# Two of a pair's four sums of weight blocks made by DMA

## The chip, the cores and the metric

The kernel runs on one core of a Trainium2 chip. The time is the device time of one execution in microseconds (us); the median of several executions is compared.

## The reference

The reference is a small decoder trunk for 512 positions of width 1024 in float32: a recurrent layer (Griffin RG-LRU) and a layer of stick-breaking attention, with a feed-forward block ahead of and behind each. The four feed-forward blocks are what the change is about. Each computes, for a hidden width of 2816,

```python
def swiglu(h, w13, w2):
    gate, up = jnp.split(h @ w13, 2, axis=-1)
    return (jax.nn.silu(gate) * up) @ w2
```

on an RMS-normed `h`, and half of the result is added to the residual stream.

## The kernel before, in words

Everything is kept transposed: 128 partitions of features by 512 positions. A product in float32 precision is made of three passes of TensorE: a weight tile is split into a high part (`hi`, rounded to the format that TensorE takes) and a low part (`lo`, the raw tile minus `hi`), the activations likewise, and `hi*hi`, `hi*lo` and `lo*hi` are added up in PSUM.

The hidden width of a feed-forward block is cut into 22 columns of 128, taken in three parts of 8, 8 and 6 (`THIRDS`). Some first columns of a block are computed plainly (`PLAIN`: 6, 4, 0 and 4 in the four blocks). All others are taken two at a time, as **pairs**: gate and up of two columns form one matrix, which is multiplied by Strassen's scheme in Winograd's form with seven products of half size instead of eight (`pair`, `FORMS`). There are 37 pairs. Behind each third stand the eight down products with `w2`.

A pair's seven weights are called forms and are used in the order a11, a12, s2, s3, s1, a22, s4. Four of them would be blocks of the weights (a11, a12, a22, and a21, which is only used in sums); the sums are s1 = a21 + a22, s2 = s1 + a11, s3 = a11 + a21 and s4 = s2 + a12 (`SUMS`). A block is a tile of 128x1024 float32, 512 KB. For each form the engines do this:

- SP's queue loads the block from HBM (L109), or VectorE adds two tiles (L114);
- ScalarE casts the tile to `hi` (L85), VectorE subtracts to get `lo` (L89);
- TensorE does 24 matmuls of 128x256 with them (L201).

The results of the forms are gathered in three PSUM banks, X, Y and Z. The forms a11, s2, s1 and s4 all add to bank X; between them ScalarE or VectorE takes out what has been added up so far (L389 to L399), then come Silu (L401, L402), the product of gate and up (L403, L404) and the split of the activations (L409, L410).

`Weights` deals out the tiles. Its plan lists all weights in the order of use. `get` returns the next one, and before that it emits loads, sums and splits of those ahead: in the feed-forward blocks up to four ahead. When a pair's first form is emitted, `block` issues all four loads of the pair at once and makes the sums when their form is asked for. Raw tiles come from two pools that have seven buffers together (three and four), `hi` and `lo` from pools of five; a load or a sum waits until a buffer of its pool is free. The order of instructions on each engine is laid down when the program is built, by a scheduler that goes by data dependences, free buffers and the order of emission; on the chip each engine works its list off in that order. GpSimd works at the start, in the recurrent layer, with k and q, and in attention; its casts of weights (L87) and subtraction (L89) belong to the start and to those layers.

Of the kernel before, what the change touches and what calls it, by code (L numbers as in the profile page):

```python
# [10 lines left out]
ALU = mybir.AluOpType  # L11
# [11 lines left out]
BLOCKS = ("a11", "a21", "a22", "a12")  # L23
SUMS = {"s3": ("a11", "a21"), "s1": ("a21", "a22"), "s2": ("s1", "a11"), "s4": ("s2", "a12"), **{b: None for b in BLOCKS}}
# [24 lines left out]
class Weights:  # L49
# [53 lines left out]
    def block(self, j, name, src):  # L103

        g = self.group
        if not g:
            for k, b in enumerate(BLOCKS):
                g[b] = self.tile(j, "w_raw", f"w_{b}_{j}")
                self.nc.sync.dma_start(g[b], src[k])  # L109
        if name not in g:  # L110
            p, q = SUMS[name]
            p, q = (self.block(j, t, src) for t in (p, q))
            g[name] = self.tile(j, "w_raw", f"w_{name}_{j}")
            self.nc.vector.tensor_tensor(out=g[name], in0=p, in1=q, op=ALU.add)  # L114
        return g[name]
# [960 lines left out]
```

## Time and profile before

| | |
|---|---|
| median of 3 runs | 1880.0 us (1879.47 to 1881.92) |
| the profiled execution, its own time | 1879.02 us |
| its span, first to last instruction | 1877.3 us |
| mean granted clock of TensorE | 0.994 of full speed |
| TensorE busy | 1839.0 us |
| VectorE busy | 1382.4 us |
| ScalarE busy | 921.7 us |
| GpSimd busy | 156.6 us |
| moved by DMA | 207.87 MB |

The profile is of one execution. In its rows PE is TensorE's matmuls, PEld its weight loads, DVE is VectorE, ACT ScalarE, POOL GpSimd, SP the engine whose queue issues the loads (SPq). A row of an instruction shows `out<-in` by the names of the tiles, shapes as partitions x elements, `xN` for N of them, and in brackets the idle time of the engine just before it with what ended it. `w_a` is a tile with a block, `w_s` one with a sum, `w_hi` and `w_lo` the split parts. Times in a row of the timeline count from the start of the span.

### The profile page before, as it was taken

Reading aid. Unit: us, or ns where it says so; the run is one execution under the profiler, and the core shown is the slowest. Engines: PE = TensorE matmul, PEld = TensorE weight load, DVE = VectorE, ACT = ScalarE, POOL = GpSimd, SP = SyncE. Lnnn points to the kernel's source line nnn. Section 1 sums busy time; section 2 is a strip of 40 time slices with the busy share of each in tenths; the row PEclk is TensorE's granted clock in tenths of the full one; section 3 lists DMA queues with packets and bytes.
Section 4 is the critical chain, followed back from the end, with each engine's and each line's share of the span. In section 5 each row is a group of like instructions: output and inputs, shape, how many; then the busy total and the mean of one; then the engine's idle time right before and its main releaser. Section 6 shows DMA issues by size and latency. Waiting matters only on the chain.

```text
span 1877.3 us, 27297 instructions
## 1 busy us (share of the span) xinstructions
PE 1839.0 (98%) x11040; PEld 1633.1 (87%) x11040; DVE 1382.4 (74%) x1709; ACT 921.7 (49%) x1282; POOL 156.6 (8%) x196
## 2 busy tenths in 40 slices
PE   9999999999999999999899999999898999999999
PEld 7889989778789899997689899898676789899897
DVE  8958657698788586576978667585799879667483
ACT  6525435368555254354545335254588745345251
POOL 1000000032000000000200000000365500000000
PEclk9999999999999999999999999999999999999999
DMA  6223423222415134232474324134365431425131
GB/s 225 91 79 98 139 71 98 79 79 82 154 46 179 46 101 124 90 93 76 135 213 126 111 79 146 56 111 148 117 188 154 147 92 46 146 79 157 57 109 61
DMA packets 73118, 207.87 MB, mean 111 GB/s; under 512 B 7584, under 2 KB 17056, under 8 KB 72480
## 3 DMA queue, kind: packets, MB, share of 16 engines
q1 hardware_dynamic: 72704, 205.81, 35.3%
q8 instruction: 86, 1.41, 0.3%
q10 hardware_dynamic: 288, 0.32, 0.1%
q14 instruction: 40, 0.33, 0.1%
HBM read 189.85 MB, written 16.25 MB: 110 GB/s over the span
## 4 chain that ended last, share of the span: by engine, by line
PE 44%; DVE 5%; issue 3%; POOL 2%; ACT 1%; SPq 0%; DMA 0%; POOLq 0%; DVEq 0%; ACTq 0%
PE pdffn L201 13%; PE pXffn L201 12%; PE pYffn L201 6%; PE pZffn L201 3%; PE v L201 2%; PE wo L201 2%; PE k L201 2%; PE puffn L201 1%; PE pgffn L201 1%; DVE spl L862 1%; PE z L201 1%; DVE t L862 1%; DVE sp L852 1%; POOL sph L859 0%; DVE w_lo L89 0%
## 5 line engine op out<-in xcount | busy, mean ns | idle before, releaser
L85 ACT CAST w_hi<-w_raw 128x1024 fp32r<-128x1024 f32 (+1 forms) x165 | 165.7, 1007 | 256.5 <-PE pdffn L201 82.5
L85 ACT CAST w_hi<-w_s 128x1024 fp32r<-128x1024 f32 x148 | 155.2, 1050 | 254.0 <-PE pdffn L201 105.4
L89 DVE TENSOR_TENSOR w_lo<-w_raw,w_hi 128x1024 fp32r<-128x1024 f32 (+3 forms) x191 | 219.9, 1154 | 76.8 <-ACT w_hi L85 68.2
L201 PE MATMUL pXffn<-hhffn,w_hi 128*128 128x256 f32 x832 | 235.5, 283 | 0.3 <-ACT effn L389 0.3
L201 PE MATMUL pXffn<-hlffn,w_hi 128*128 128x256 f32 x832 | 235.5, 283 | 0.0
L201 PE MATMUL pXffn<-hhffn,w_lo 128*128 128x256 f32 x832 | 235.5, 283 | 0.0
L201 PE MATMUL pdffn<-ahffn,w_hi 128*128 128x512 f32 x592 | 230.8, 390 | 0.3
L201 PE MATMUL pdffn<-alffn,w_hi 128*128 128x512 f32 x592 | 230.7, 390 | 0.0
L201 PE MATMUL pdffn<-ahffn,w_lo 128*128 128x512 f32 x592 | 230.4, 389 | 0.0
L89 DVE TENSOR_TENSOR w_lo<-w_s,w_hi 128x1024 fp32r<-128x1024 f32 x148 | 180.8, 1221 | 33.1 <-ACT w_hi L85 33.0
L85 ACT CAST w_hi<-w_a 128x1024 fp32r<-128x1024 f32 x111 | 116.5, 1050 | 171.4 <-PE pdffn L201 70.2
L89 DVE TENSOR_TENSOR w_lo<-w_a,w_hi 128x1024 fp32r<-128x1024 f32 x111 | 135.5, 1222 | 36.2 <-ACT w_hi L85 34.8
L201 PEld LDWEIGHTS pXffn<-hhffn,w_hi 128*128 128x128 f32 x832 | 159.7, 192 | 0.8 <-ACT effn L389 0.5
L201 PEld LDWEIGHTS pXffn<-hlffn,w_hi 128*128 128x128 f32 x832 | 159.7, 192 | 0.3
L201 PEld LDWEIGHTS pXffn<-hhffn,w_lo 128*128 128x128 f32 x832 | 159.7, 192 | 0.0
L453 DVE SCALAR_TENSOR_TENSOR x<-pdffn,x 128x512 f32<-128x512 f32 x72 | 49.8, 691 | 141.2 <-PE pdffn L201 141.2
L201 PEld LDWEIGHTS pdffn<-ahffn,w_hi 128*128 128x128 f32 x592 | 111.2, 188 | 24.6 <-ACT ahffn L409 1.8
L201 PEld LDWEIGHTS pdffn<-alffn,w_hi 128*128 128x128 f32 x592 | 111.2, 188 | 24.4 <-DVE alffn L410 1.1
L201 PEld LDWEIGHTS pdffn<-ahffn,w_lo 128*128 128x128 f32 x592 | 111.2, 188 | 22.7
L201 PE MATMUL pYffn<-hhffn,w_hi 128*128 128x256 f32 x416 | 117.7, 283 | 0.0
L201 PE MATMUL pYffn<-hlffn,w_hi 128*128 128x256 f32 x416 | 117.7, 283 | 0.0
L201 PE MATMUL pYffn<-hhffn,w_lo 128*128 128x256 f32 x416 | 117.7, 283 | 0.0
(1154 smaller groups left out, 4691.7 us busy)
## 6 DMA issues: line engine op xcount, KB each, us to landing
w_a<-in_ffn_s SPq DMA_DIRECT2D x148, 512.0 KB, 3.7
w_raw<-in_ffn_w SPq DMA_DIRECT2D x90, 512.0 KB, 4.5
w_raw<-in_ffn_w SPq DMA_DIRECT2D x32, 384.0 KB, 3.4
w_raw<-in_w_in SPq DMA_DIRECT2D x16, 512.0 KB, 3.6
qp<-qd SPq DMA_DIRECT2D x14, 512.0 KB, 5.5
w_raw<-in_w_out SPq DMA_DIRECT2D x8, 512.0 KB, 3.8
w_raw<-in_w_k SPq DMA_DIRECT2D x8, 512.0 KB, 3.6
w_raw<-in_w_v SPq DMA_DIRECT2D x8, 512.0 KB, 3.7
```

The costliest lines, as they stand in the source:

```text
L85: nc.scalar.copy(out=hi[:, cs], in_=raw[:, cs])
L89: eng.tensor_tensor(out=lo[:, cs], in0=raw[:, cs], in1=hi[:, cs].bitcast(F32), op=ALU.subtract)
L201: nc.tensor.matmul(o, l, r, start=start, stop=stop, skip_group_check=True)
L453: nc.vector.scalar_tensor_tensor(out=x[m], in0=pd, scalar=0.5, in1=x[m], op0=ALU.mult, op1=ALU.add)
L852: nc.vector.scalar_tensor_tensor(out=self.sp, in0=self.z, scalar=0.0, in1=ee, op0=ALU.max, op1=ALU.add)
L862: nc.vector.tensor_tensor(out=lo, in0=src, in1=hi.bitcast(F32), op=ALU.subtract)
```

## The change

When a pair's first form is emitted, five tiles are loaded in place of four, in the order a11, a12, s1, a22, s3. The tile of s1 is loaded with a21, and a DMA on GpSimd's queue then reads a22 from HBM and adds it to the tile; the tile of s3 is loaded with a11, and a second DMA adds a21. The sums s2 and s4 stay adds on VectorE. No tile holds a21 any more, so a pair has seven raw tiles instead of eight. From HBM a pair reads seven blocks instead of four.

```diff
@@ -104,12 +104,15 @@
         g = self.group
         if not g:
-            for k, b in enumerate(BLOCKS):
+            for b in ("a11", "a12", "s1", "a22", "s3"):
                 g[b] = self.tile(j, "w_raw", f"w_{b}_{j}")
-                self.nc.sync.dma_start(g[b], src[k])
+                p, q = SUMS[b] or (b, None)
+                self.nc.sync.dma_start(g[b], src[BLOCKS.index(p)])
+                if q:
+
+                    self.nc.gpsimd.dma_start(g[b], src[BLOCKS.index(q)], accum_op=ALU.add)
         if name not in g:
-            p, q = SUMS[name]
-            p, q = (self.block(j, t, src) for t in (p, q))
+            p, q = (g[t] for t in SUMS[name])
             g[name] = self.tile(j, "w_raw", f"w_{name}_{j}")
             self.nc.vector.tensor_tensor(out=g[name], in0=p, in1=q, op=ALU.add)
         return g[name]
```

## Rows read from the trace of the kernel before

**Rows 1.** The page: span; busy time, share of the span and instructions by engine.

```profile
span 1877.3 us, 27297 instructions
...
PE 1839.0 (98%) x11040; PEld 1633.1 (87%) x11040; DVE 1382.4 (74%) x1709; ACT 921.7 (49%) x1282; POOL 156.6 (8%) x196
```

**Rows 2.** By stretch: length; PE, PEld, DVE, ACT, POOL busy; clock, DMA share, GB/s.

```profile
520.00:835.00 315.00, 314.74 (x2098) 291.11 (x2097) 226.30 (x258) 141.40 (x178) 0.00 (x0) 1.00 0.31 96
835.00:971.00 136.00, 128.10 (x546) 103.17 (x545) 104.86 (x149) 66.85 (x99) 14.02 (x16) 0.97 0.43 136
...
1572.00:1840.00 268.00, 268.00 (x1893) 252.84 (x1892) 186.06 (x195) 115.02 (x143) 0.00 (x0) 1.00 0.34 107
...
1011.38:1031.54 20.16, 20.16 (x170) 20.16 (x170) 17.06 (x19) 10.86 (x15) 0.00 (x0) 1.00 0.35 106
```

**Rows 3.** Chain that ended last, in two stretches: start us, us, what.

```profile
1008.50 5.76 PE pXffn L201 x48
...
1017.14 2.88 PE pXffn L201 x24
...
1598.02 2.88 PE pXffn L201 x24
```

**Rows 4.** Timeline of ScalarE in an ordinary pair and in a pair behind plain columns.

```profile
1015.07 0.58 ACT L389 COPY effn<-pXffn 128x512 f32<-128x512 f32 x1
...
1028.62 1.05 ACT L85 CAST w_hi<-w_s 128x1024 fp32r<-128x1024 f32 x1 [1.83 <-PE pYffn L201]
...
1031.51 1.05 ACT L85 CAST w_hi<-w_s 128x1024 fp32r<-128x1024 f32 x1 [1.10 <-PE pXffn L201]
...
1590.11 1.05 ACT L85 CAST w_hi<-w_s 128x1024 fp32r<-128x1024 f32 x1 [4.34 <-DVE w_s L114]
...
1595.06 1.05 ACT L85 CAST w_hi<-w_a 128x1024 fp32r<-128x1024 f32 x1 [0.92 <-PE pXffn L201]
...
1597.05 0.57 ACT L389 COPY effn<-pXffn 128x512 f32<-128x512 f32 x1
```

**Rows 5.** Groups by line: sums of two blocks; busy us, mean ns, idle us before and its releasers.

```profile
L114 DVE TENSOR_TENSOR w_s<-w_a,w_a 128x1024 f32<-128x1024 f32 x74 | 90.0, 1221 | 13.4 <-DMA w_a<-in_ffn_s 11.3 <-issue 1.4
```

**Rows 6.** Waits of SP's queue: waiting line, what ended it, us, times, longest us.

```profile
SPq L109 <- DVE w_lo L89: 539.3, 98, 21.3
```

**Rows 7.** Timeline of SP's queue ahead of the pairs at 1031.54 and 1592.27.

```profile
1004.00 7.13 SPq L109 DMA_DIRECT2D w_a<-in_ffn_s  x4
...
1007.96 0.33 SPq L109 DMA_DIRECT2D w_a<-in_ffn_s  x1
...
1572.57 9.01 SPq L109 DMA_DIRECT2D w_a<-in_ffn_s  x4
...
1579.55 0.80 SPq L109 DMA_DIRECT2D w_a<-in_ffn_s  x2
1579.93 1.65 SPq L109 DMA_DIRECT2D w_a<-in_ffn_s  x2
```

**Rows 8.** Groups on GpSimd: busy us, mean ns, idle us before and its releasers.

```profile
L87 POOL TENSOR_SCALAR w_hi<-w_raw 128x1024 fp32r<-128x1024 f32 x17 | 20.0, 1176 | 706.4 <-PE pdffn L201 678.2 <-issue 11.5 <-PE q L201 9.3
...
L675 POOL TENSOR_SCALAR thk<-tk 128x512 fp32r<-128x512 f32 x8 | 7.5, 944 | 419.6 <-ACT tk L672 419.6
...
L89 POOL TENSOR_TENSOR w_lo<-w_raw,w_hi 128x1024 fp32r<-128x1024 f32 x1 | 2.7, 2677 | 0.1
...
L324 POOL TENSOR_SCALAR o0h<-o 128x512 fp32r<-128x512 f32 x1 | 0.6, 615 | 0.0
```

**Rows 9.** The tile `w_a`: time from issue to landing of its loads.

```profile
DMA to landing us min/median/max: 3.2/3.7/7.1
```

**Rows 10.** Timeline of VectorE in the pair from 1011.38.

```profile
1015.41 1.23 DVE L114 TENSOR_TENSOR w_s<-w_a,w_a 128x1024 f32<-128x1024 f32 x1 [1.42 <-issue]
...
1020.62 1.22 DVE L114 TENSOR_TENSOR w_s<-w_s,w_a 128x1024 f32<-128x1024 f32 x1
...
1028.70 0.69 DVE L399 TENSOR_TENSOR effn<-pYffn,effn 128x512 f32<-128x512 f32 x1 [0.58 <-PE pYffn L201]
```

## The prediction

> **What bounds the kernel now.** I read the page first: of a span of 1877.3 us TensorE is busy 1839.0, VectorE 1382.4, GpSimd 156.6 [rows 1]. A busy share is an average over unlike stages, so next I cut the span into stretches [rows 2]. Where the pairs run, TensorE is busy all the time: 314.74 of 315.00 us in one feed-forward block, 268.00 of 268.00 in the last, 20.16 of 20.16 in a single pair, at a granted clock of 1.00, the upper of its two levels (2.4 GHz). What it idles lies elsewhere, for instance in the k and v products (128.10 of 136.00), where the change edits nothing. The chain of waits shows why [rows 3]: in a pair one form of 24 matmuls follows the other at 2.88 us, and seven make 20.16 us. So in the 37 pairs TensorE is the bound, and VectorE, with 17.06 us of work in those 20.16 [rows 2], lies beside it.
>
> One order must still be seen, for ScalarE works in line. It casts the raw blocks and also copies the first form out of its PSUM bank (L389). TensorE's third form adds to that same bank, so the copy has to be done before it starts. In the pair that starts at 1011.38, halfway through the first row of [rows 3], the copy starts at 1015.07 and takes 0.58 us [rows 4]; the third form starts at 1017.14: 1.49 us to spare. A late cast ahead of a copy in ScalarE's line is thus the way from a late block to TensorE.
>
> **What is removed.** Two of four adds per pair, those of two blocks: 74 at 1.221 us, 90.0 us of VectorE [rows 5]. They lie where TensorE has no idle time to give back (0.26 us in the stretches read), so I take 0. Their tiles go or move too: 7 raw tiles per pair where there were 8, over the same 7 buffers. The last sum of a pair no longer waits for a buffer of its own pair, and SP's loads, which wait mostly for VectorE's splits to free one (539.3 us in 98 waits) [rows 6], should start no later than now.
>
> **What is added: one load.** Five loads of 512 KB per pair on SP's queue in place of four. An issue is 0.33 us [rows 7], five are 1.65 of 20.16; SP waits for buffers anyway. Four loads now keep the 16 DMA engines 0.35 busy over a pair [rows 2], 1.76 us of all engines per load; the fifth makes it 0.44.
>
> **What is added: two accumulating DMAs on GpSimd's queue.** GpSimd does nothing in the stretches with pairs [rows 2]; its next casts wait for the down products in any case (678.2 us) [rows 8]. Behind a waiting accumulation stands only the other one. It waits first for its load to land: 3.7 us from issue, median, 7.1 at most [rows 9]. Then GpSimd has to issue, which no row shows: from 0.33 us, SP's issue [rows 7], to 2.7, GpSimd's longest operation on a tile of 128x1024; I take 1.2, what its cast of such a tile takes [rows 8]. The transfer, which reads two operands and writes one, no row shows either: no less than a plain load, 3.7 us; at most two of the slowest loads end to end, 14.2. I take 2 x 3.7 = 7.4, two ordinary transfers, the nearest to the work. So issue and transfer are 8.6 us (bounds 4.0 and 16.9). On the engines an accumulation at one to two plain loads brings a pair's share from 0.44 to between 0.61 and 0.79: no queue fills up.
>
> **Is that hidden?** Take the pair that runs from 1031.54, 20.16 after the one above. Its four loads go out from 1004.00 on, the third at 1007.96 [rows 7]. Put in that place, s1 is summed at 1007.96 + 3.7 + 8.6 = 1020.3, just ahead of where s2's add stands, 1020.62 [rows 10]. The fifth load (for s3) can have its buffer by 1015.41, when the first sum takes one today [rows 10]: 1015.41 + 12.3 = 1027.7, and its cast is at 1028.62 [rows 4]. A later cast is absorbed too: before its next cast ScalarE idles 1.10 us [rows 4], and the copy has its 1.49 to spare, together 2.6. Issue and transfer may so take 1028.62 + 2.6 - 1015.41 - 3.7 = 12.1 us before TensorE waits. Cost in an ordinary pair: 0.
>
> Tightest is the second pair behind the plain columns, which two feed-forward blocks have in the same form; I read the later one. Its loads come at 1572.57 and then three from 1579.55 on, the second of these at 1579.93 [rows 7], and ScalarE already waits 4.34 us for a sum before 1590.11 [rows 4]. A third load at 1579.93 makes s1 at 1592.2 and s2 at 1593.5, its cast 3.4 us late. Behind it stand 0.92 us of idle time and the copy, which ends at 1597.62, 0.40 ahead of the third form [rows 3, 4]: TensorE would lose 3.4 - 0.92 - 0.40 = 2.1 us. Against that, its buffers come free earlier, since the first pair's last sum needs none of them. Bounds 0 to 2.1, two places; I take 0.5 each, nearer to 0 because of those buffers: 1.0 us.
>
> A rule for such a transfer stands in the Trainium skill, "Collectives: The Full Stack", Part 3, under the bandwidth ceiling: the add itself is free, and the second source read halves the rate. By it one load's engine time comes on top, an estimate of 3.7 + 1.76 = 5.5 us for the transfer, and the term of the tight pairs would be at most 0.1 us each instead of 2.1; no run here shows it yet.
>
> **Sum.** Span 1877.3 plus 1.7 around it is the profiled execution's 1879.02; with 1.0 it is 1880.0. The median of the runs lies 0.98 above the profiled one, so the forecast is 1881.0 us: no change that can be told, since a measurement of this kernel can tell about 0.2%, 3.8 us.
>
> **Rivals.** (a) Slower: the sums by DMA come late, the cast waits in ScalarE's line, and the PSUM copy behind it holds TensorE. It decides when issue and transfer pass 12.1 us in an ordinary pair. For it: no row shows such a transfer, VectorE's adds waited for a landing 11.3 us in all even now [rows 5], and there are the two tight pairs. Against: the 3.5 us between 8.6 and 12.1. Price: each us past the point is 37 us, so one is 1918; at the bound of 16.9 it is 4.8 x 37 = 178, 2059. Chance 0.32.
>
> (b) Slower by GpSimd held off: could it write its descriptors only while VectorE is idle, an accumulation that is ready at 1015.41 would wait until the gap ahead of 1028.70, that is 1028.12, for VectorE works through until then [rows 10]. That is 12.7 + 7.4 = 20.1 us, 8.0 past the point, and 37 x 8.0 = 296: about 2177. Against it: GpSimd's casts of 128x512 take 615 ns in one place and 944 in another [rows 8], a third of a us of disturbance and no block. Chance 0.04. The Trainium skill has such a rule ("SBUF — State Buffer", the section on the two separate sides): VectorE in a mode with two ports keeps GpSimd from writing a DMA's descriptors. Its section on who interferes with whom exempts two-operand adds and subtractions, and these are most of what VectorE runs here; by that the rival falls away.
>
> (c) Faster: VectorE's freed time reaches TensorE. The only idle time near a sum is the 7.90 us in the stretch that ends where the first pair without plain columns begins [rows 2]; to be told, over 3.8 of it would have to come back, 1872 to 1876. Against: the sums stand at the end of that stretch, and the idle time is spread over the products ahead. Chance 0.07.
>
> **How the numbers follow.** No change 0.57, (a) 0.32, (b) 0.04, (c) 0.07. The likeliest case alone spans 1877 to 1884. The range goes down to 1874, into (c), and up to 1920, one us per pair, which takes in about half of (a): some 0.2 is left out. Faster 0.07, same 0.57, slower 0.36.
>
> **What would show it.** Right: VectorE's sums of two blocks are gone and 74 adds are left; a pair still takes TensorE 20.16 us, without idle time; the DMA share of a pair is between 0.6 and 0.8; an accumulation takes less than 12 us from its wait to its landing. Wrong: ScalarE's casts wait long for sums or for a DMA, and TensorE's third form for the copy of L389. A pair longer than 20.16 us breaks the forecast.

## The result and the profile after

With the change the kernel takes **1939.56 us** (median of 4 runs, 1936.96 to 1949.27) against 1880.49 of the kernel before in the same session: a ratio of 1.0323, 95% interval 1.0297 to 1.035. That is 59 us slower, outside the range of the prediction. The profiled execution is the longest of the four (1949.27 us, span 1947.5), 70.2 us longer in span than the one shown before. In the rows of after, L201 has become L204, and L389 to L410 have moved down by 3; L110 issues the loads of the blocks, L113 the accumulating DMAs, L117 makes the sums on VectorE.

First the page of after: span, busy times, the two large DMA queues, and the issues with size and median time from issue to landing.

```profile
span 1947.5 us, 27548 instructions
...
PE 1860.2 (96%) x11040; PEld 1649.7 (85%) x11040; DVE 1297.0 (67%) x1635; ACT 922.5 (47%) x1282; POOL 220.2 (11%) x270
...
q1 hardware_dynamic: 78032, 225.21, 37.5%
q0 software_dynamic: 10656, 38.80, 12.1%
...
w_a<-in_ffn_s SPq DMA_DIRECT2D x111, 512.0 KB, 4.1
...
w_s<-in_ffn_s SPq DMA_DIRECT2D x74, 512.0 KB, 4.4
w_s<-in_ffn_s POOLq DMA_DIRECT2D x74, 512.0 KB, 5.9
```

VectorE lost 74 adds and 85.4 us of work (1382.4 in [rows 1]), as the change says. TensorE has as many matmuls as before and is busy 21.2 us longer, in a span that is 70.2 us longer: so some 49 us are new idle time, and 21 are matmuls that take longer. The stretches show both; the columns are those of [rows 2].

```profile
140.00:300.00 160.00, 151.45 (x1072) 143.03 (x1072) 92.36 (x99) 67.06 (x82) 9.51 (x11) 0.99 0.56 147
540.00:860.00 320.00, 309.45 (x2062) 286.82 (x2061) 201.87 (x235) 136.01 (x172) 14.75 (x17) 0.99 0.52 135
1085.00:1330.00 245.00, 231.21 (x1527) 215.01 (x1527) 133.77 (x143) 90.89 (x111) 12.11 (x14) 0.97 0.53 134
...
161.43:184.76 23.33, 20.41 (x171) 20.21 (x170) 14.78 (x16) 9.96 (x13) 1.72 (x2) 1.00 0.60 158
1025.34:1054.22 28.88, 22.19 (x171) 21.78 (x170) 18.35 (x20) 15.32 (x20) 1.73 (x2) 0.88 0.58 148
```

Where pairs run, TensorE is no longer gapless: it stands still 8.55 us of 160, 13.79 of 245. The last two rows are one pair each, taken from its second form (a12, the first into bank Z) to the second form of the next pair; this took 20.16 us before [rows 2]. One lost 3.2 us by idling; the other lost 6.7 by idling and 2.0 more because its matmuls ran at a granted clock of 0.88 on average: TensorE stands still from 1028.4 to 1033.9, and from 1031 to 1037 the clock is 0.50, the lower of its two levels (1.2 GHz). Over the whole program the clock went from 0.994 to 0.983, and 0.011 x 1947.5 = 21 us, about the busy time that was added. The DMA share of 0.60 is over a pair of 23.33 us; over 20.16 us the same transfers would be 0.69, within the forecast's 0.61 to 0.79.

What TensorE waits for, and what that waits for, stands in the list of waits of after: line, what ended the wait, us in total, times, longest.

```profile
POOL w_s L113 <- DMA w_s<-in_ffn_s: 369.1, 29, 44.3
...
DVE w_s L117 <- DMA w_s<-in_ffn_s: 93.5, 17, 8.3
...
ACT w_hi L85 <- DVE w_s L117: 55.5, 17, 5.8
...
PEld pXffn L204 <- DVE effn L400: 43.1, 20, 4.8
...
PE pXffn L204 <- DVE effn L400: 39.0, 19, 4.5
...
ACT w_hi L85 <- DMA w_s<-in_ffn_s: 15.6, 6, 9.2
...
PEld pXffn L204 <- ACT effn L392: 9.1, 2, 5.8
```

In 20 of the 22 waits of its weight loads at bank X it is not the copy that the prediction watched (L392, formerly L389) but **L400**, VectorE's subtraction out of bank X. It has to be done before the pair's last form, s4, adds to that bank. The two waits for the copy lie in the first two pairs of the block without plain columns; the pair from 1025.34 is the second of them. And VectorE waits 93.5 us, in 17 places, at L117 for an accumulating DMA. How the two are joined is seen in the timeline of after, in the pair from 161.43 above.

```profile
161.36 0.33 SPq L110 DMA_DIRECT2D w_s<-in_ffn_s  x1
...
161.94 0.86 POOL L113 DMA_DIRECT2D w_s<-in_ffn_s  x1 [17.26 <-DVE alffn L413]
...
165.71 0.86 POOL L113 DMA_DIRECT2D w_s<-in_ffn_s  x1 [2.91 <-DVE effn L398]
...
165.52 1.23 DVE L89 TENSOR_TENSOR w_lo<-w_s,w_hi 128x1024 fp32r<-128x1024 f32 x1 [0.25 <-ACT w_hi L85]
173.62 1.23 DVE L117 TENSOR_TENSOR w_s<-w_s,w_a 128x1024 f32<-128x1024 f32 x1 [6.87 <-DMA w_s<-in_ffn_s]
174.76 1.22 DVE L89 TENSOR_TENSOR w_lo<-w_a,w_hi 128x1024 fp32r<-128x1024 f32 x1
175.90 1.22 DVE L117 TENSOR_TENSOR w_s<-w_s,w_a 128x1024 f32<-128x1024 f32 x1
177.03 1.22 DVE L89 TENSOR_TENSOR w_lo<-w_a,w_hi 128x1024 fp32r<-128x1024 f32 x1
178.17 0.68 DVE L400 TENSOR_TENSOR effn<-pXffn,effn 128x512 f32<-128x512 f32 x1
```

The first accumulation makes s3 and the second, 3.77 us later, makes s1, whose load is the row of SP's queue. Both rows name an instruction of VectorE in their brackets, but GpSimd waits for the load: in after 73 of the 74 issues start 0.5 to 0.8 us behind the landing of their own load, and one 1.2. VectorE stands still for 6.87 us at the add of s2 = s1 + a11 **of the next pair**, until s1 has landed; behind it in VectorE's line stand two splits, the add of s4 and, last, the L400 that the present pair needs. In the kernel before the same stretch has the same order on VectorE (and the add of s3 as well), with nothing to wait for:

```profile
166.68 1.22 DVE L114 TENSOR_TENSOR w_s<-w_s,w_a 128x1024 f32<-128x1024 f32 x1
...
170.20 1.23 DVE L114 TENSOR_TENSOR w_s<-w_s,w_a 128x1024 f32<-128x1024 f32 x1
171.34 1.22 DVE L89 TENSOR_TENSOR w_lo<-w_a,w_hi 128x1024 fp32r<-128x1024 f32 x1
173.13 0.69 DVE L397 TENSOR_TENSOR effn<-pXffn,effn 128x512 f32<-128x512 f32 x1 [0.56 <-PE pXffn L201]
```

There the subtraction starts at 173.13, in after at 178.17: 5.0 us later at nearly the same place in the program (its pair began 0.1 us later). TensorE loses 3.2 of them; 1.8 were to spare.

The order on SP and GpSimd explains why s1 is so late. The list in `block` asks for s1 third and s3 last. But a load goes where its buffer frees, and the tiles go in turn to a pool of three and one of four buffers. In 18 of the 37 pairs the order laid down has s3's load, and s3's accumulation, ahead of s1's (the expectations below say 17). Comparing the starts of the pairs in both traces pair by pair, some 48 of the 71 us lie just ahead of 16 pairs. These are 16 of the 18 with s3 first; the other two are the first pairs behind plain columns. In the 16 the way from the issue of s1's load to the landing of its sum takes 10.2 to 14.2 us, median 11.8 (161.36 to 173.59 in the pair shown). About 23 us are elsewhere: 8.7 and 5.2 in the first pairs of the block that has no plain columns, 7.4 in the second pair behind plain columns in one block, and small ones.

### The profile page after: what moved, and what is told of

Its sections match the earlier page's. It is cut to its first block, busy times and chain, and to the rows that moved or that the text cites. A ratio compares the mean times of both kernels' runs of the same rounds, so it can differ in the third digit from the quotient of the medians.

```text
span 1947.5 us, 27548 instructions
## 1 busy us (share of the span) xinstructions
PE 1860.2 (96%) x11040; PEld 1649.7 (85%) x11040; DVE 1297.0 (67%) x1635; ACT 922.5 (47%) x1282; POOL 220.2 (11%) x270
## 3 DMA queue, kind: packets, MB, share of 16 engines
q0 software_dynamic: 10656, 38.80, 12.1%
## 5 line engine op out<-in xcount | busy, mean ns | idle before, releaser
L204 PE MATMUL pXffn<-hhffn,w_hi 128*128 128x256 f32 x832 | 240.1, 289 | 24.1 <-DVE effn L400 24.1
L204 PE MATMUL pXffn<-hlffn,w_hi 128*128 128x256 f32 x832 | 238.6, 287 | 0.0
L204 PE MATMUL pXffn<-hhffn,w_lo 128*128 128x256 f32 x832 | 238.5, 287 | 0.0
L204 PE MATMUL pdffn<-ahffn,w_hi 128*128 128x512 f32 x592 | 230.8, 390 | 0.3
L204 PE MATMUL pdffn<-alffn,w_hi 128*128 128x512 f32 x592 | 230.8, 390 | 0.0
L204 PE MATMUL pdffn<-ahffn,w_lo 128*128 128x512 f32 x592 | 230.4, 389 | 0.0
L113 POOL DMA_DIRECT2D w_s<-in_ffn_s x74 | 64.2, 868 | 1211.7 <-DMA w_s<-in_ffn_s 369.1
L204 PEld LDWEIGHTS pXffn<-hhffn,w_hi 128*128 128x128 f32 x832 | 162.9, 196 | 27.1 <-DVE effn L400 26.7
L117 DVE TENSOR_TENSOR w_s<-w_s,w_a 128x1024 f32<-128x1024 f32 x74 | 90.5, 1223 | 121.9 <-DMA w_s<-in_ffn_s 93.5
L204 PEld LDWEIGHTS pXffn<-hlffn,w_hi 128*128 128x128 f32 x832 | 163.0, 196 | 0.4
L204 PEld LDWEIGHTS pXffn<-hhffn,w_lo 128*128 128x128 f32 x832 | 162.9, 196 | 0.0
L204 PEld LDWEIGHTS pdffn<-alffn,w_hi 128*128 128x128 f32 x592 | 111.1, 188 | 24.6 <-DVE alffn L413 1.1
L204 PEld LDWEIGHTS pdffn<-ahffn,w_hi 128*128 128x128 f32 x592 | 111.1, 188 | 24.6 <-ACT ahffn L412 1.8
L204 PEld LDWEIGHTS pdffn<-ahffn,w_lo 128*128 128x128 f32 x592 | 111.1, 188 | 22.5
L204 PE MATMUL pXffn<-hhn,w_hi 128*128 128x256 f32 x352 | 104.9, 298 | 23.7 <-DVE effn L400 14.9
```

The costliest lines, as they stand in the source:

```text
L113: self.nc.gpsimd.dma_start(g[b], src[BLOCKS.index(q)], accum_op=ALU.add)
L204: nc.tensor.matmul(o, l, r, start=start, stop=stop, skip_group_check=True)
```

## Experiments

The theories: **ORDER**, later split into LINE and LATE: the accumulations are as cheap as thought, but the order in which they are issued and waited for puts a late one ahead of work that TensorE needs. **TRAFFIC**: the 58 MB more from HBM and the accumulations' load on the DMA engines slow what else moves. Medians are over all runs; the ratio is to the kernel before on the same chip.

**s1 first in its pair.**

```diff
-            for b in ("a11", "a12", "s1", "a22", "s3"):
+            for b in ("s1", "a11", "a12", "a22", "s3"):
```

> The changed kernel with the tile of s1 at the head of the pair's list of loads, so that its load and its accumulation stand ahead of those of s3 in all 37 pairs (in the changed kernel they stand behind s3's in 17). Theory ORDER (s1 is needed first and summed last; s2's add waits for it in VectorE's line, and the subtraction of L400 behind it keeps TensorE): the 48 us lost in front of those pairs go, the 22 us at the start of two blocks may stay: 1885 to 1908 us. Theory TRAFFIC (three more blocks per pair read from HBM make all transfers late, whichever comes first): 1930 to 1945 us as before.

Measured: 1910.75 us, 1.0165 (1.0145 to 1.0184), 3 us above the range of ORDER and so a miss, though a small one. Same DMAs, half of the loss gone. VectorE's subtraction no longer stops TensorE; what does, in the list of waits of this kernel, is the copy:

```profile
ACT w_hi L85 <- DMA w_s<-in_ffn_s: 37.1, 6, 10.1
...
PEld pXffn L204 <- ACT effn L392: 20.2, 5, 6.6
PE pXffn L204 <- ACT effn L392: 19.2, 5, 6.4
```

That is the route of the prediction's rival (a): s3, the fifth load, gets its buffer late, ScalarE's cast waits for its accumulation, and the copy L392 stands behind the cast. It holds in five places, each among the first four pairs of a block.

**Only the order of the two accumulations.** Loads stay as built; s1's accumulation is put ahead of s3's on GpSimd.

```diff
-                    self.nc.gpsimd.dma_start(g[b], src[BLOCKS.index(q)], accum_op=ALU.add)
+                    i = self.nc.gpsimd.dma_start(g[b], src[BLOCKS.index(q)], accum_op=ALU.add)
+                    if b == "s1":
+                        first = i
+                    else:
+                        self.tc.add_manual_dep(i.ins, first.ins.name, self.nosync, reason="s1 first")
...
+    W.tc, W.nosync = tc, NOSYNC
```

> The changed kernel with one thing laid down: on GpSimd's queue the accumulation of s1 stands ahead of that of s3; loads and buffers stay in their order, so s1's load still starts late in 17 pairs. ORDER: s1 no longer shares the engines with s3's accumulation and is summed some 2 to 3 us earlier, about half of the 48 us goes: 1905 to 1928 us. TRAFFIC: 1930 to 1945 us.

Measured: 1912.93 us, 1.0176 (1.016 to 1.0191). The order alone is worth 27 us. The rest is again mostly VectorE's subtraction (20.8 us in 15 waits of the weight loads): s1's load is still issued behind s3's.

**s3 alone by DMA**, s1 back on VectorE.

```diff
-            for b in ("a11", "a12", "s1", "a22", "s3"):
+            for b in ("a11", "a21", "a22", "a12", "s3"):
...
-            p, q = (g[t] for t in SUMS[name])
+            p, q = (self.block(j, t, src) for t in SUMS[name])
```

> Only s3 is summed by DMA, s1 is an add on VectorE as in the kernel before; six blocks per pair are read in place of seven. ORDER: s3 feeds no add, only its own cast, so VectorE's line never waits for an accumulation: 1878 to 1895 us. TRAFFIC: two of the three additional blocks remain, so about two thirds of the 59 us remain: 1910 to 1925 us.

Measured: 1886.66 us, 1.0042 (1.0026 to 1.0059). An accumulation a pair costs 6.6 us in the whole program if it is the one that no sum on VectorE waits for.

**s1 alone by DMA**, s3 back on VectorE, is its counterpart.

```diff
-            for b in ("a11", "a12", "s1", "a22", "s3"):
+            for b in ("a11", "a12", "s1", "a22", "a21"):
```

> The changed kernel with s1 alone made by DMA and s3 back on VectorE (loads a11, a12, s1, a22, a21): one accumulation a pair, and one raw tile more a pair. s3 alone by DMA cost 0.42%. LINE: the sum that is needed first and is followed by a sum on VectorE carries the cost, but without a second accumulation beside it it lands some 2 us earlier: 1885 to 1925 us. If the number of accumulations decided and not which one: as for s3 alone, 1883 to 1890 us.

Measured: 1928.26 us, 1.026 (1.0233 to 1.0287), 3 us above the range that LINE had, again a small miss. With as many accumulations as in the run before it costs some seven times as much (48 against 6.6 us). So it is not the number of accumulations that decides, but which sum is late. Its waits name the same line as after:

```profile
DVE w_s L117 <- DMA w_s<-in_ffn_s: 72.6, 19, 7.7
...
PEld pXffn L204 <- DVE effn L400: 24.9, 13, 3.7
```

**Traffic without accumulation**: the kernel before, with three plain loads of 512 KB more per pair on GpSimd's queue, into a tile that nothing reads.

```diff
                 self.nc.sync.dma_start(g[b], src[k])
+            for k in range(3):
+                t = self.more.tile([P, 1024], F32, tag="junk", name=f"junk{k}_{j}", bufs=1)
+                self.nc.gpsimd.dma_start(t, src[k])
```

> The kernel before, its four adds on VectorE unchanged, and per pair three additional plain loads of 512 KB on GpSimd's queue into a tile that nothing reads. ORDER: 1876 to 1886 us, no change. TRAFFIC: 1915 to 1945 us.

Measured: 1901.9 us, 1.0118 (1.01 to 1.0136): neither theory's figure. Of the 19 us of span that it is longer, 14 are lost ahead of the first pair, where the additional loads, which wait for nothing but their own tile, run ahead of the program and meet the loads of the start. Among the pairs it loses 4.7 us, 4.5 of them in the first pair of the block without plain columns, whose additional loads start only 26 us ahead of it. The others run 30 to 230 us ahead of the pair to which they belong. So this shows that the bytes don't stop the other pairs; it does not show what they would do in their pair's own time.

**The second DMA without the add.**

```diff
-                    self.nc.gpsimd.dma_start(g[b], src[BLOCKS.index(q)], accum_op=ALU.add)
+                    self.nc.gpsimd.dma_start(g[b], src[BLOCKS.index(q)])
```

> The changed kernel, each second DMA still on GpSimd's queue, in its place and behind its load, but as a plain load that overwrites the tile instead of adding to it (so s1 becomes a22 and s3 becomes a21; the two sums are left out). It tells the price of the add in the transfer from the price of the second step. The accumulation landed 5.9 us after its issue and a plain load there 4.0, so each second step ends some 2 us earlier, two in flight together some 3. ORDER: 16 pairs lost 48 us, 3.0 us each; most of that is then covered, but not all: 1890 to 1920 us. LONG (a rival: the add's extra time is the whole cause): 1878 to 1888 us. If the waiting for the first load alone decides: 1925 to 1940 us.

Measured: 1894.19 us, 1.0082 (1.0066 to 1.0099). The built order of loads and second DMAs is the one of after, down to the last pair, and three quarters of the loss are gone. The page of this kernel beside that of after above gives the price of the add in the transfer:

```profile
q0 software_dynamic: 10656, 38.80, 6.4%
...
L113 POOL DMA_DIRECT2D w_s<-in_ffn_s x74 | 39.4, 533 | 1181.9 <-DMA w_s<-in_ffn_s 366.9
...
w_s<-in_ffn_s POOLq DMA_DIRECT2D x74, 512.0 KB, 4.3
```

The time of the 16 DMA engines per DMA goes from 6.4% x 1891.0 / 74 = 1.64 us to 12.1% x 1947.5 / 74 = 3.18 us, the time to landing from 4.3 to 5.9 us. So most of the loss needs both, the order and the longer DMA.

**No second DMA at all.**

```diff
-                if q:
-
-                    self.nc.gpsimd.dma_start(g[b], src[BLOCKS.index(q)], accum_op=ALU.add)
```

> The changed kernel without its second DMAs: five loads per pair in the same built order, and s1 is a21, s3 is a11 (the two sums are left out). What is left of the change are the fifth load, seven tiles a pair and s3's load ahead of s1's in 17 pairs. ORDER (a late second step holds s2's add, and VectorE's line behind it): without a second step s1 is there some 7 us earlier, 1878 to 1888 us. If the fifth load or the buffers themselves hold TensorE, or if VectorE's new order does: 1900 us or more.

Measured: 1881.23 us, 1.0013 (1.0003 to 1.0022). Five loads, seven tiles and s3's load ahead of s1's cost about 2 us (0.6 to 4.1 by the interval): what was taken for the fifth load (nothing) holds within that.

**An eighth raw buffer.**

```diff
-        bufs = dict(w_raw=4, w_hi=2, w_lo=2)
+        bufs = dict(w_raw=5, w_hi=2, w_lo=2)
```

> The changed kernel with one raw buffer more: the pool of the later tiles holds five instead of four, so eight tiles of 512 KB stand where seven stood. Loads, accumulations and adds are the same in number and size. The built order then has s1's load and s1's accumulation ahead of s3's in all pairs but one. ORDER (the second step starts late, because loads wait for a buffer and s3 goes ahead of s1; 48 of the 71 us by s1 behind s3, the rest by late buffers): 1879 to 1892 us. TRAFFIC (the accumulations themselves, 58 MB more read and the doubled engine time, delay whatever else moves): nothing of that is taken away, 1925 to 1945 us.

Measured: 1911.12 us, 1.0171 (1.0155 to 1.0186): **missed**. The order on SP and GpSimd became the one of the list in all pairs but one, as the expectation says of the built order, and still 32 us are lost. The timeline of this kernel shows a second form of the same trap, ahead of the pair whose second form starts at 1052.59:

```profile
1024.03 0.86 POOL L113 DMA_DIRECT2D w_s<-in_ffn_s  x1 [11.86 <-DMA w_s<-in_ffn_s]
...
1030.70 1.23 DVE L117 TENSOR_TENSOR w_s<-w_s,w_a 128x1024 f32<-128x1024 f32 x1 [5.53 <-issue]
1031.85 0.42 DVE L407 SCALAR_TENSOR_TENSOR effn<-pXffn,effn 128x256 f32<-128x256 f32 x1
...
1032.30 1.14 ACT L412 CAST ahffn<-effn 128x512 fp32r<-128x512 f32 x2 [6.04 <-DVE effn L407]
1033.34 0.58 ACT L392 COPY effn<-pXffn 128x512 f32<-128x512 f32 x1
```

Since the tiles are free earlier, the add of s2 is now laid so early that it stands ahead of L407, the last product of the pair two before. VectorE waits 5.53 us there, until 6.67 us after the accumulation's issue. The row names no releaser, but that is when the accumulation of s1 lands (1030.62). L407 is late, so ScalarE's L412 is, and the copy L392 behind it holds TensorE, which then loses 4.7 us. The theory that only the order of s3 and s1 matters falls with this run; what is common to both is the place of s2's add in VectorE's line.

**Control for the buffer**: the same line in the kernel before.

> The kernel before (all four sums on VectorE) with the same eighth raw buffer: what the buffer is worth without the change. ORDER and TRAFFIC both: TensorE idles nowhere in a pair there, so 1876 to 1884 us, no change that can be told. If the buffer alone moves the time, e5 has to be compared with this run and not with the kernel before.

Measured: 1883.87 us, 1.0025 (1.0015 to 1.0036), 4.6 us more by the buffer alone, so 27 of the 32 us remain on the change's account.

**Only the line of VectorE.** All loads and accumulations stay as they are, s3 ahead of s1 in 18 pairs; s2's add is put behind the subtraction L400 of the pair before.

```diff
-            self.nc.vector.tensor_tensor(out=g[name], in0=p, in1=q, op=ALU.add)
+            i = self.nc.vector.tensor_tensor(out=g[name], in0=p, in1=q, op=ALU.add)
+            if name == "s2" and self.mark is not None:
+                self.tc.add_manual_dep(i.ins, self.mark.ins.name, self.nosync, reason="behind the pair before")
...
+    W.tc, W.nosync, W.mark = tc, NOSYNC, None
...
-                    nc.vector.tensor_tensor(out=e[:, 2], in0=ps, in1=e[:, 2], op=ALU.subtract)
+                    W.mark = nc.vector.tensor_tensor(out=e[:, 2], in0=ps, in1=e[:, 2], op=ALU.subtract)
```

> The changed kernel with one rule more for the order on VectorE: the add that makes s2 stands behind the subtraction out of bank X of the pair before (in the changed kernel it stands ahead of it in the pairs with s3 ahead of s1). All loads and accumulations keep their size and their built order, s3 ahead of s1 in 17 pairs. LINE (the accumulations only cost because a late one is waited for ahead of the subtraction in VectorE's line; s2's form comes some 11 us after its cast, so the sum itself is early enough): the 48 us of the 16 pairs go for the most part, the 22 us of late buffers stay, 1885 to 1912 us. LATE (the sum itself comes too late for its form, wherever it is waited for): 1925 to 1945 us.

Measured: **1888.05 us, 1.0043** (1.0028 to 1.0058). 51 of the 59 us are gone. The timeline of the same pair as above (lines are 3 further down, L403 is after's L400) and the stretch from 140 to 300:

```profile
162.75 0.86 POOL L113 DMA_DIRECT2D w_s<-in_ffn_s  x1 [17.38 <-DMA w_s<-in_ffn_s]
165.40 0.86 POOL L113 DMA_DIRECT2D w_s<-in_ffn_s  x1 [1.79 <-DVE alffn L416]
...
173.04 0.69 DVE L403 TENSOR_TENSOR effn<-pXffn,effn 128x512 f32<-128x512 f32 x1 [0.72 <-PE pXffn L206]
173.65 2.47 DVE L117 TENSOR_TENSOR w_s<-w_s,w_a 128x1024 f32<-128x1024 f32 x2
```

```profile
140.00:300.00 160.00, 160.00 (x1165) 152.40 (x1164) 99.70 (x105) 70.21 (x87) 9.50 (x11) 1.00 0.57 152
```

s1's accumulation is issued at 165.40, much as in after (165.71), lands at 173.39 (173.59), and the sum is made at 173.65 (173.62 in after). It is hardly earlier and not shorter. But the subtraction now starts at 173.04 and TensorE is busy 160.00 of 160.00 us, with the clock at 1.00 and more DMA traffic a second than in after. None of the 16 pairs loses anything any more: the sum itself was in time, it was waited for in the wrong place. The run also bounds TRAFFIC, in the pairs' own time: every load and accumulation of after is still there, and 7.7 us of the 59 are left for all else together.

**Control for the line**: the same rule in the kernel before.

> The kernel before (all four sums on VectorE) with the same rule for VectorE's order as in the run of the line order: s2's add behind the subtraction out of bank X of the pair before. There every sum is made on VectorE from blocks that lie there, so nothing waits long at the add in either place. LINE: 1878 to 1886 us, the rule by itself is worth nothing, and what the run of the line order won back was the waiting for the accumulation. If the rule by itself made the kernel faster, or slower: below 1876 or above 1888 us, and the run of the line order has to be compared with this one.

Measured: 1881.11 us, 1.0007 (0.9998 to 1.0016): the rule by itself brings nothing.

**Both mends of the loads**, s1 first and an eighth buffer.

> The changed kernel with both mends: s1's load first in its pair and an eighth raw buffer. s1 first alone left 28 us, all from s3's late accumulation (fifth load, late for a buffer); the buffer alone left 32 us, from s2's add of the next pair and from s3. LINE: each mend takes the other's rest, 1880 to 1893 us, so that the two sums by DMA cost next to nothing and bring nothing. TRAFFIC or LATE (two accumulations a pair of 5.9 us each hold the pairs in any order): 1905 us or more.

Measured: 1895.77 us, 1.0084 (1.0069 to 1.0099): between the two figures and therefore a miss for LINE. Of 17 us lost among the pairs, 14.8 lie in the first two pairs of the block without plain columns, where the buffers come free late. The first of these two lost 4.2 to 8.5 us in every run that made both sums by accumulation, whatever the order; the second lost nothing in three of them (s1 first; the eighth buffer; VectorE's line).

## Why the prediction was wrong

**The bound, and the adds removed at 0**: right. VectorE lost 85 us of work and no run gained anything by it; where no late sum is in the way, TensorE is as gapless as before.

**The fifth load at 0**: right, the run without second DMAs is 0.13% above before (0.03 to 0.22).

**The accumulating DMA**: taken at 8.6 us for issue and transfer (bounds 4.0 to 16.9); it measures 5.9 from issue to landing, 0.87 of that the issue, and up to 8.8 when two are in flight (7.9 in the pair shown). From the issue of the load to the landing of the sum the forecast had 3.7 + 8.6 = 12.3 us; the 16 pairs that lost time have a median of 11.8. This unknown price, on which rival (a) was hung, was thus no larger than forecast, and the kernel still lost 59 us. The nearness of 11.8 to 12.3 is partly luck: the sum left out the 0.5 us between landing and issue, and had the transfer too long (7.4, where 5.9 - 0.87 = 5.0 was measured).

**The rule cited** from the Trainium skill, "Collectives: The Full Stack", Part 3 (the add is free, the second source read halves the rate): the runs agree, 3.18 us of the DMA engines against 1.64 for a plain one of the same size. By the estimate of 5.5 us made from it the tight pairs would have cost next to nothing; the median transfer measured is shorter still, 5.0 (5.8 for s1 of the tight pair that lost 7.4). So the transfer's length alone does not account for that loss.

**"Put in that place", the third load, for all pairs**: this is one of two steps that failed. The pair that was worked out is one where it holds: s1's sum came in time and it lost nothing. But the order of loads was argued from the list in the diff, for one pair, and [rows 7] show only plain blocks. In 18 pairs the buffer of the third tile frees later than the one of the last, and s3 goes ahead. With it "start no later than now" fails: the third load went out 23.6 us ahead of its pair (1031.54 - 1007.96), while s1's load in those 16 pairs of after goes out 18.5 to 24.0 ahead, although most of these pairs start late themselves. Where nothing is lost, in the run of VectorE's line, s1 lands 4.2 to 7.6 us ahead of the same 16 pairs, and the prediction had 11.2 (1031.54 - 1020.3).

**"A late cast ahead of a copy in ScalarE's line is thus the way"**: the other step that failed, and the dearer one. There are two in-order lines between a block and TensorE. VectorE makes s2 from s1, and subtracts out of bank X at L397 before the last form; [rows 10] show s2's add at 1020.62, well inside the pair before. With s1 made on VectorE that place costs nothing, since what it waits for stands right ahead of it in the same line. Made by DMA, it becomes a wait at the head of a full line. In after, L400 follows the add by 178.17 - 173.62 = 4.55 us in the pair shown, so what s1 lands late goes to TensorE, but for the 1.8 us that L400 had to spare there. The prediction asked by how much a *cast* could be late (2.6 us for s3's, and s2's in the tight pairs) and put s1 just ahead of s2's add, 1020.3 against 1020.62; it did not ask what stands behind that *add*. The run of VectorE's line shows the price of that: 51 us. The prices of the two steps overlap and don't add up: the order of the accumulations alone was worth 27 us.

**Rival (a)** at 0.32 named the right kind of trap, a late sum at the head of an in-order line. Its place (ScalarE's copy) carries only a small part in after, 9.1 us of waits against 43.1 by L400; with s1 first it carries most of what is left. Its point of decision, 12.1 us of issue and transfer, was never reached; the chain from load to sum was about as long as forecast and started late. That 1939.56 lies between its two prices, 1918 and 2059, is luck. **Rival (b)**, GpSimd held off by VectorE, fell: GpSimd issues an accumulation in 0.86 us beside VectorE's work, and 0.5 to 0.8 us behind the landing of its load in all cases but one. **Rival (c)** did not come about.

**The tight second pairs behind plain columns**, 0.5 us each: one of the two places lost 7.4 us, the other 0.5. The 7.4 come by L400 again: s2's add waits 3.68 us for s1 ahead of it, in a pair whose accumulations are in the order s1, s3. With VectorE's line mended 0.5 are lost there too, but the second pair itself then loses 2.0 at its third form, by the copy (L395 in that run; the other such pair loses nothing), and with s1 first the two lose 7.7 and 4.4 in that way. So in those runs place and way are the prediction's and 0.5 each was too small; in after the loss by L400 comes ahead of the pair, and its third form waits for nothing.

**TensorE's clock** was left out: stops cost more than their length. Of the 70 us of the profiled execution 21 are busy time at a lower granted clock.

What stays open: 7.7 us (0.43%) that remain by the medians with VectorE's line mended, 9.5 in the span of the profiled execution. Half of these (4.8) lie in the first pair of the block without plain columns, where ScalarE's copy stands behind two writes of v (L749) that wait for DMAs of v to HBM:

```profile
978.68 0.69 ACT L749 ACTIVATE vh<-v,rc 128x512 fp32r<-128x512 f32 x1 [4.64 <-DMA vd<-vh]
...
981.70 0.69 ACT L749 ACTIVATE vh<-v,rc 128x512 fp32r<-128x512 f32 x1 [1.40 <-DMA vd<-vh]
982.28 0.58 ACT L395 COPY effn<-pXffn 128x512 f32<-128x512 f32 x1
```

The last eight of these DMAs take 5.7 us in the median against 3.0 in the kernel before. The run of traffic without accumulation has such waits too (4.41 and 2.17 us) and loses 4.5 us in the same pair. So in this one pair additional traffic alone can hold TensorE; what part of the 4.8 is due to it, and what to late sums ahead in ScalarE's line, no run tells apart.

No kernel here was faster than the one before, and none can be expected to be by these sums while TensorE is gapless in the pairs.

## What to carry to other kernels

When a value that an engine makes itself is handed to a DMA, list every instruction on every engine that takes it, and for each ask what stands behind it in that engine's line: an instruction that was free because its operand stood just ahead of it becomes a wait that holds all the rest. Read the order that was laid down for all repetitions of a pattern, not the order of a loop in the source and not that of one instance, and where the new value is late, first try moving its reader behind what the bottleneck needs. Work that is taken off an engine which is not the bound brought nothing in any run here, so a change like this could at best break even.

## What the runs showed of the hardware

A DMA that adds 512 KB of float32 from HBM to a tile took 3.18 us of the 16 DMA engines against 1.64 for one that overwrites, 5.9 us against 4.3 to landing, and 0.87 us against 0.53 of GpSimd for its issue. With two in flight the longest in after took 8.8 us. GpSimd's issue began 0.5 to 0.8 us behind the landing it waited for in 73 of 74 cases. A stop of TensorE of a few us was followed in some pairs by matmuls at a lower granted clock (0.88 on average over the pair from 1025.34, with 2.0 us more of busy time), and in others not (1.00 in the pair from 161.43).
